# Routed layers: the last two experts' outputs stay on chip and are added by float32 products; the branch stands ahead of them

## The chip, the cores and the metric

One core of a Trainium2 chip. The program runs on that core alone; the time is the device time of one execution in microseconds (us), and the kernel before was run three times. TensorE (PE) multiplies, VectorE (DVE) and ScalarE (ACT) work on elements, GpSimd (POOL) and SyncE (SP) mostly issue DMAs here. Each engine works through its own instructions in order and waits on semaphores.

## What is computed

256 tokens of 1024 values pass a first block (feed-forward, retention and forgetting attention, feed-forward; two layers), and then a second block of two routed layers: `a` (window attention; 256 latent and 256 context tokens, 512 in all, four tiles of 128) and `b` (differential attention; 256 tokens, two tiles). After its attention each routed layer has a mixture of 16 experts, two for a token, a residual with `ALPHA`, and a layer norm:

```python
def moe_ffn(h, w_router, router_bias, w_gate, w_up, w_down):
    ...
    gates = (jax.nn.one_hot(eid, N_EXPERTS, dtype=F32) * w[..., None]).sum(1)
    out = jnp.zeros_like(h)
    for e in range(N_EXPERTS):
        y = (jax.nn.silu(h @ w_gate[e]) * (h @ w_up[e])) @ w_down[e]
        out = out + gates[:, e:e + 1].astype(h.dtype) * y
    return out
```

All weights are float32. A weight block of 128x1024 (0.5 MB) is used once.

## The kernel before

**The stream of weights.** `Stream` (L150 to 215) loads weight blocks in the order of their use. `_issue` starts a load into a buffer `raw` (SP's queue, L177), `_conv` makes two rounded halves of a block: `whi` by a cast on ACT (L189) and `wlo` by a subtraction on DVE (L191). `mm3` (L335 to 337) then multiplies three times: high by high, high by low, low by high. `DEPTHS` says by stage how many blocks may be in flight (`nraw`), converted and unreleased (`nhalf`), and converted ahead (`ahead`). `between()`, which products call between blocks, converts one block ahead and runs one piece of other work from the list `fill`. The order of instructions on each engine is the order in which the program is written.

**The routed experts.** `moe` routes the tokens, scatters their rows to `X` in memory by expert slots (`scatter`, L1733), and goes through the 16 experts in the order `ORDER[l]`. Experts are ranked by their number of tokens; a rank has a fixed number of slots (up to 256, down to 32), and tokens beyond them are overflow. For an expert, `xcol` multiplies its tokens with four blocks of the gate and four of the up weights; `folded` and `trans` turn the result into `uT`, `hth` and `htl`; its down product `Dn` (four blocks) runs one iteration later, so that the down product of an expert stands behind the gate and up products of the next. A small expert (64 or 32 slots) multiplies both of its halves at once (L1777, `mm<-whi,xt` and `mm<-wlo,xt`).

**How outputs reach the tokens.** `Dn` copies its accumulator to `y` (ACT, L1824) and stores it to `Y` in memory (L1825); the last expert in two halves (L1829, L1830). Then comes `overflow` (L1978, L1979): every engine loads the number of overflow blocks and branches. It is zero for these inputs, so each jumps over the block; SP, which waits in it for all of its DMA lanes, lets the others go on. Then `combine` has POOL gather each token's two rows from `Y` (`yr`, L1919), ACT scale the one by its gate (L1930), and DVE add the other with its gate (L1935), multiply by the row `g2` (L1936), add to `x` with `ALPHA` (L1939) and take the statistics (L1940). Thirteen small products make the layer norm's factors (L302 to 313, L1948, L1949). After layer a `attn_b` scales the first tile (L2046), transposes it, and goes on; after layer b `second` scales and shifts (L2232, L2236) and stores the result.

The inner part of the combination, before:

```python
            def both(c):
                a, b = y[i, 0], res["b"]
                V.scalar_tensor_tensor(a[:, c], a[:, c], g[:, 0, i:i + 1], b[:, c], op0=OP.mult, op1=OP.add)
                V.tensor_tensor(a[:, c], a[:, c], self.g2[t // 2][:, c], op=OP.mult)

            def added(c):
                V.scalar_tensor_tensor(x[:, c], x[:, c], ALPHA, y[i, 0][:, c], op0=OP.mult, op1=OP.add)
                V.bn_stats(st[:, c.start // 512, :], x[:, c])
```

Of the kernel before, what the change touches and what calls it, by code (L numbers as in the profile page):

```python
# [18 lines left out]
try:  # L19
# [38 lines left out]
def layout(pairs):  # L58
# [4 lines left out]
    for p, ranks in enumerate(pairs):  # L63
# [15 lines left out]
        for r, _ in ranks:  # L79
# [11 lines left out]

N4, N2 = 35, 21
# [6 lines left out]
          "route": ((6, 5, 5), (10, 5, 5)), "moe": ((6, 7, 5), (10, 7, 5)), "more": ((10, 11, 8), (11, 11, 8)), "end": (2, 6, 6)}  # L99
# [5 lines left out]
def host_constants():  # L105
    f = np.float32
    c = {}
    c["eye"] = np.eye(128, dtype=f)
    tri = (np.arange(128)[:, None] <= np.arange(128)[None, :]).astype(f)
    c["cum"] = np.concatenate([np.zeros((128, 128), f), tri, np.ones((128, 128), f)], 1)  # L110
    c["causal"] = np.where(tri.T > 0, f(0), f(NEG))
    inv = np.power(f(10000.0), -np.arange(0, 128, 2, dtype=f) / f(128))
    ang = np.arange(SEQ, dtype=f)[:, None] * inv[None, :]
    cs, sn = np.cos(ang), np.sin(ang)
    c["rope"] = np.stack([np.concatenate([cs, cs], 1), np.concatenate([-sn, sn], 1)], 1)
    lg = np.log1p(-np.exp2(-5.0 - np.arange(4)))
# [17 lines left out]
    c["rest"] = np.array(SLOTS)[:, None, None] + 128 * np.arange(8).reshape(2, 4) + np.arange(128)[:, None, None, None]  # L134
# [110 lines left out]
class Kernel:  # L245
# [647 lines left out]
    def zeros(self):  # L893

        z = self.k4([128, D], name="zero")
        self.nc.gpsimd.memset(z, 0.0)
        for x, m in zip(self.X, SLOTS):
            for a in range(0, m, 128):
                self.nc.gpsimd.dma_start(x[a:a + 128, :], z)
                yield  # L900
        for y, m, n, runs in zip(self.Y, SLOTS, MORE, RUNS):
            gaps = [(p * 256 + r[-1][0] + r[-1][1] * r[-1][2], p * 256 + 256) for p, r in enumerate(runs)]
            for a, b in gaps + [(m + a * 128, m + a * 128 + 128) for a in range(n)]:
                if a < b:
                    self.nc.gpsimd.dma_start(y[a:b, :], z[:b - a])
                    yield

    def ada_setup(self):
        self.mod = self.dr.tile([DEPTH, 2, 6, D], FT, name="mod")
        self.Y = [self.dr.tile([m + n * 128, D], FT, name=f"Y{m}") for m, n in zip(SLOTS, MORE)]  # L910

        self.X = [self.dr.tile([m + 1024, D], FT, name=f"X{m}") for m in SLOTS]
        self.H = [self.dr.tile([n, D], FT, name=f"H{n}") for n in (512, 256)]
# [470 lines left out]
    def attn_out(self, l, tiles, vec):  # L1384
# [84 lines left out]
        def second(oT):  # L1469
# [23 lines left out]
            def split(t):  # L1493
                self.split(h2[t][0], h2[t][1], hs[t])
                i = tiles.index(t)
                nc.gpsimd.dma_start(self.H[l][i * 128:i * 128 + 128, :], hs[t])
# [185 lines left out]
    def one_hot(self, r, i, c0, n, out):  # L1682

        V = self.nc.vector
        a = self.t([128, 256], "oha", bufs=2)
# [6 lines left out]
        V.scalar_tensor_tensor(out, self.iota[:, :n], rm[:, 1:2], a[:, :n], op0=OP.is_equal, op1=OP.add)  # L1692

    def moe(self, l, h2, hs):
# [30 lines left out]
        def scatter():  # L1725

            rows = self.t([128, 2, 4], "rtrow")[:, :, :T]
            V.tensor_tensor(rows, r, self.rest[:, l, :, :T], op=OP.min)
            ri = self.t([128, 2, 4], "rtrowi", I32)[:, :, :T]
# [72 lines left out]
        def stored(e, i, p, n):  # L1802
            hT[e, i] = (self.k2([128, 4, n], FR, name="hth"), self.k2([128, 4, n], FR, name="htl"))
            self.split(hT[e, i][0], hT[e, i][1], p)

        def Dn(e):
# [12 lines left out]
            for i, (c, n, _, _) in enumerate(ts):  # L1819
                rows = Y[p * 256 + c:p * 256 + c + n, :]  # L1820
                if e != seq[-1]:
# [3 lines left out]
                    S.dma_start(rows, y[:n])  # L1825
                else:
                    for x in range(2):
                        y = self.k2([128, 512], name="y")
                        S.copy(y[:n], b[i][x][:n])  # L1829
                        S.dma_start(rows[:, x * 512:(x + 1) * 512], y[:n])  # L1830
                del hT[e, i]

# [12 lines left out]
        for j, e in enumerate(seq):  # L1845
            p, ts = place[e][0], TILES[l][e]
            nxt = pairs[got] if j + 1 < len(seq) and got < len(pairs) and place[seq[j + 1]][0] == pairs[got] else None
            if j == len(seq) - 2:
                self.g2 = {v: self.modrow(l, v, 5) for v in range(T // 2)}
            if nxt is not None:  # L1850
# [45 lines left out]
            if last is not None or nxt is not None:  # L1896
                for i in range(len(ts)):
                    trans(i)
            else:
                self.fill.extend([lambda: None] + [lambda i=i, f=trans: f(i) for i in range(len(ts))])  # L1900
# [5 lines left out]
        if MORE[l] and not self.dbg.get("noov"):  # L1906
            self.overflow(l, Y)
        return g

    def combine(self, l, g):  # L1910
# [5 lines left out]
        for i in range(T):  # L1916
            for j in range(2):
                y[i, j] = self.k4([128, D], name="yr")
                nc.gpsimd.indirect_dma_start(out=y[i, j], out_offset=None, in_=self.Y[l],  # L1919
                                             in_offset=bass.IndirectOffsetOnAxis(ap=self.ri[:, j, i:i + 1], axis=0))  # L1920
        halves = [slice(0, 512), slice(512, 1024)]

        def pieces(i, t):
# [14 lines left out]
            def added(c):  # L1938
                V.scalar_tensor_tensor(x[:, c], x[:, c], ALPHA, y[i, 0][:, c], op0=OP.mult, op1=OP.add)  # L1939
                V.bn_stats(st[:, c.start // 512, :], x[:, c])  # L1940

            def norm():

                del y[i, 0], res["b"]
# [5 lines left out]
            p = [scaled]  # L1950
            for c in halves:
                p += [lambda c=c: both(c), lambda c=c: added(c)]
            return res, p, norm
# [20 lines left out]
    def overflow(self, l, Y):  # L1974
# [4 lines left out]
        with self.tc.If(n > 0):  # L1979
            oi = self.owners()  # L1980
            for a in range(MORE[l]):
# [3 lines left out]
                for i in range(T):  # L1985
                    self.one_hot(self.rt, i, first, 128, oh[:, i, :])
                x = [self.k2([128, 4, 128], name="ovx") for _ in range(2)]
                for f in range(2):
                    h = [self.k2([128, 512], name="ovt") for _ in range(T)]
                    for j in range(T):  # L1990
                        nc.sync.dma_start(h[j], self.H[l][j * 128:j * 128 + 128, f * 512:(f + 1) * 512])
# [34 lines left out]
    def attn_b(self, g):  # L2026
# [28 lines left out]
        comb = self.combine(0, g)  # L2055
# [18 lines left out]
        def ahead(n):  # L2074

            no = lambda: None
            first, rest, norm, done = ([lambda j=j: [f() for f in comb[j][1][0:3]] for j in range(4)],
                                       [lambda j=j: [f() for f in comb[j][1][3:5]] for j in range(4)],
                                       [lambda j=j: [f() for f in comb[j][2]()] for j in range(4)],
                                       [lambda j=j: finish(order[j], comb[j][0]) for j in range(4)])  # L2080
            step = lambda: hT[order[n + 1]].step()
            return ([lambda: (rest[1](), norm[1]()), first[2], done[1], rest[2], norm[2], step, step, done[2]],
                    [first[3], rest[3], step, step, norm[3]], [done[3], no, step, step], [])[n]

        (res, p, norm), p1 = comb[0], comb[1][1]
# [6 lines left out]
        p1[0]()  # L2092
# [3 lines left out]
        for f in p1[1:3]:  # L2096
# [118 lines left out]
    def second(self):  # L2215
# [5 lines left out]
        g = self.moe(0, *h2)  # L2221
        del h2
        h2 = self.attn_b(g)
        del self.xs[2:]
        g = self.moe(1, *h2)
        lg, lb = self.row(self.I["ln_ffn_g_2"][1:2, :]), self.row(self.I["ln_ffn_b_2"][1:2, :])
        comb = self.combine(1, g)
        (r0, p0, n0), (r1, p1, n1) = comb

# [10 lines left out]
        for f in p0 + p1[0:1]:  # L2240
            f()
        self.weave(n0(), p1[1:])
# [86 lines left out]
```

## Time and profile before

| | |
|---|---|
| runs, us | 2428.07, 2427.30, 2422.94 (median 2427.3) |
| the profiled execution | 2428.2 us; its span, from first to last instruction, 2426.4 |
| PE busy | 2204.8 us (91%) |
| DVE busy | 1830.1 us (75%) |
| ACT busy | 1269.2 us (52%) |
| POOL busy | 258.7 us (11%) |
| HBM read and written | 512.67 and 41.50 MB, 228 GB/s over the span |

Times in rows are microseconds from the start of the span. Experts of layer a run from about 1480 to 1800, those of layer b from about 2080 to 2392. In a row of the timeline stand the start, the busy time of a group of like instructions, the engine, the line and operation, what it writes and reads, how many, and in brackets how long the engine was idle before it and what ended that. A `q` behind an engine's name is its sequencer, which issues DMAs and branches.

### The profile page before, as it was taken

The numbers are of one execution on the slowest core, as the hardware profiler recorded it, in microseconds if no ns is written. First come the engines' busy times: TensorE is split into PE (matmuls) and PEld (weight loads), VectorE is DVE, ScalarE is ACT, GpSimd is POOL, SyncE is SP. The second block draws the span as 40 slices with busy tenths as digits, with TensorE's granted clock in tenths as the row PEclk, the third lists the DMA queues.
The fourth block names the chain that finished last, engine by engine and source line by source line (L and its number), as shares of the span: only waits on it lengthen the run. The fifth ranks groups of instructions, "written<-read, shape, count | busy, mean of one in ns | idle before, by whom it ended". The sixth has DMA issues, their size and how long they took to land. (4 is left out here: it accounts for less than half of the span.)

```text
span 2426.4 us, 32170 instructions
## 1 busy us (share of the span) xinstructions
PE 2204.8 (91%) x10767; PEld 1761.5 (73%) x10767; DVE 1830.1 (75%) x2700; ACT 1269.2 (52%) x1887; POOL 258.7 (11%) x600
## 2 busy tenths in 40 slices
PE   7999999999999999999998996999958977799994
PEld 5888787788788889788876775777637855576662
DVE  5787678877877766877667766989866486778896
ACT  4445444444444545444336614878855352577783
POOL 2003101100200301120100022000020011100000
PEclk9999999999999999999999996999989998799997
DMA  8786557779798676798711136999991410899994
GB/s 276 241 238 199 158 165 228 236 232 300 243 325 252 207 226 193 245 263 234 217 53 44 53 105 245 361 371 391 385 308 39 127 63 14 330 354 339 362 396 156
DMA packets 256448, 556.44 MB, mean 229 GB/s; under 512 B 23761, under 2 KB 43153, under 8 KB 256273
## 3 DMA queue, kind: packets, MB, share of 16 engines
q1 hardware_dynamic: 233248, 481.96, 61.1%
q0 software_dynamic: 17424, 57.78, 6.5%
q10 hardware_dynamic: 5601, 14.54, 1.6%
q8 instruction: 88, 1.44, 0.3%
q14 instruction: 87, 0.71, 0.1%
HBM read 512.67 MB, written 41.50 MB: 228 GB/s over the span
## 5 line engine op out<-in xcount | busy, mean ns | idle before, releaser
L191 DVE TENSOR_TENSOR wlo<-raw,whi 128x1024 fp32r<-128x1024 f32 (+1 forms) x828 | 975.7, 1210 | 188.4 <-ACT whi L189 177.0
L189 ACT CAST whi<-raw 128x1024 fp32r<-128x1024 f32 (+1 forms) x828 | 830.4, 1043 | 190.0 <-PE mm L336 56.0
L335 PE MATMUL mm<-whi,xth 128*128 128x512 f32 (+3 forms) x1152 | 446.4, 388 | 9.2 <-ACT whi L189 5.5
L337 PE MATMUL mm<-whi,xtl 128*128 128x512 f32 (+3 forms) x1152 | 432.4, 375 | 0.1
L336 PE MATMUL mm<-wlo,xth 128*128 128x512 f32 (+3 forms) x1152 | 431.5, 375 | 0.5 <-DVE wlo L191 0.5
L335 PE MATMUL acc<-whi,hth 128*128 128x512 f32 (+4 forms) x624 | 248.0, 397 | 7.4 <-ACT hth L367 7.4
L335 PEld LDWEIGHTS mm<-whi,xth 128*128 128x128 f32 x1152 | 218.6, 190 | 47.1 <-ACT whi L189 5.9
L337 PEld LDWEIGHTS mm<-whi,xtl 128*128 128x128 f32 x1152 | 218.3, 190 | 37.1 <-DVE xtl L368 1.7
L336 PE MATMUL acc<-wlo,hth 128*128 128x512 f32 (+4 forms) x624 | 245.0, 393 | 0.2 <-DVE wlo L191 0.2
L337 PE MATMUL acc<-whi,htl 128*128 128x512 f32 (+4 forms) x624 | 244.7, 392 | 0.0
L336 PEld LDWEIGHTS mm<-wlo,xth 128*128 128x128 f32 x1152 | 218.7, 190 | 32.8 <-DVE wlo L191 1.2
L965 DVE SCALAR_TENSOR_TENSOR adaacc<-adaraw,adac,adaacc 128x512 f32<-128x512 f32 x310 | 220.7, 745 | 13.5 <-DMA adaraw<-in_w_ada_dram 11.2
L335 PEld LDWEIGHTS acc<-whi,hth 128*128 128x128 f32 (+4 forms) x624 | 107.4, 172 | 41.2 <-ACT hth L367 7.6
L337 PEld LDWEIGHTS acc<-whi,htl 128*128 128x128 f32 (+4 forms) x624 | 107.3, 172 | 36.3 <-issue 0.8
L336 PEld LDWEIGHTS acc<-wlo,hth 128*128 128x128 f32 (+4 forms) x624 | 107.4, 172 | 34.0 <-DVE wlo L191 0.6
L1777 PE MATMUL mm<-whi,xt 128*128 128x512 f32 (+1 forms) x288 | 118.2, 410 | 10.3 <-ACT xt L1723 5.8
L306 POOL TENSOR_TENSOR rsw<-rsy 128x1 f32<-128x1 f32 (+1 forms) x75 | 26.1, 349 | 867.7 <-DVE rsy L304 850.1
L1777 PE MATMUL mm<-wlo,xt 128*128 128x512 f32 (+1 forms) x288 | 116.3, 404 | 2.1 <-DVE wlo L191 2.1
L367 ACT CAST hth<-tr 128x512 fp32r<-128x512 f32 (+3 forms) x64 | 35.4, 553 | 153.0 <-PE tr L363 147.3
L335 PE MATMUL mm<-whi,hth 128*128 128x512 f32 x256 | 105.1, 411 | 5.0 <-DVE x L497 2.8
L335 PE MATMUL mm<-whi,xt 128*128 128x512 f32 (+4 forms) x256 | 102.9, 402 | 3.3 <-ACT xt L367 3.3
L336 PE MATMUL mm<-wlo,xt 128*128 128x512 f32 (+4 forms) x256 | 101.9, 398 | 3.8 <-DVE wlo L191 3.7
(471 smaller groups left out, 3344.6 us busy)
## 6 DMA issues: line engine op xcount, KB each, us to landing
raw<-in_w_ffn_in_dram SPq DMA_DIRECT2D x176, 512.0 KB, 6.0
raw<-in_w_gate_dram SPq DMA_DIRECT2D x128, 512.0 KB, 8.4
raw<-in_w_up_dram SPq DMA_DIRECT2D x128, 512.0 KB, 7.1
raw<-in_w_down_dram SPq DMA_DIRECT2D x128, 512.0 KB, 8.5
adaraw<-in_w_ada_dram SPq DMA_DIRECT2D x384, 128.0 KB, 5.5
raw<-in_w_ffn_out_dram SPq DMA_DIRECT2D x88, 512.0 KB, 5.9
raw<-in_w_in_dram SPq DMA_DIRECT2D x56, 512.0 KB, 4.2
raw<-in_wqkv_b_dram SPq DMA_DIRECT2D x24, 512.0 KB, 7.6
```

The costliest lines, as they stand in the source:

```text
L189: k.nc.scalar.copy(hi, lo)
L191: k.nc.vector.tensor_tensor(low, lo, hi.bitcast(FT), op=OP.subtract)
L306: newton = [lambda: g.tensor_tensor(w, y, y, op=OP.mult), lambda: g.tensor_tensor(w, w, a, op=OP.mult), lambda: g.tensor_scalar(w, w, -0.5 ...
L335: mm(out, xh, wh, start=first, stop=False)
L336: mm(out, xh, wl, start=False, stop=False)
L337: mm(out, xl, wh, start=False, stop=last)
L367: self.nc.scalar.copy(hi, src)
L965: V.scalar_tensor_tensor(a, r[:, i, :], sc, a, op0=OP.mult, op1=OP.add)
L1777: PE.matmul(o[:2 * n], x[:, i, c:c + 2 * n], a[:, i, :], start=first and q == 0, stop=last and q == 1)
```

## The change

The last two experts of each layer (`LAST`: ranks 11 and 12 of layer a with 64 slots each, 14 and 15 of layer b with 32 each) don't go to `Y`.

- `scaled` multiplies their accumulators by the row `g2` into an on-chip tile `zy` (128 or 64 slots in all, DVE, L1865). `gated` builds for each tile of tokens a matrix with the token's gates at the slots of its experts (L1708 to 1712), which is transposed and copied to `zgT` (L1877). `product` multiplies `zgT` with `zy` in float32 (L2012), and `last` adds the product to `x` and takes the statistics (L2016, L2017).
- `overflow` now stands ahead of the second-last expert's iteration, with its block not on the straight path of the program.
- `combine` is called when the third-last expert's down product has been stored: POOL gathers for the first two tiles, and for tile `i + 2` when tile `i` is done. Scaling, gate, row and residual of these tiles (`first`) run from `fill` in the last expert's iteration. `attn_b` and `second` get `comb` and do the rest.
- `ORDER[0]` changes so that the four experts of 64 slots come last in layer a. From the third-last expert on the stream has the depths `z`, (5, 7, 5) and (6, 8, 6), instead of (10, 11, 8) and (11, 11, 8).
- `H` and its six stores go; the overflow block would gather from `X` instead. `X` is filled with zeros in full (12 more stores of 0.5 MB, and 2 of the gaps in `Y`, at the zeros' old place in the program).

```diff
-ORDER = ((15, 9, 0, 10, 11, 1, 12, 2, 3, 4, 5, 14, 7, 6, 13, 8),
+ORDER = ((15, 14, 0, 5, 1, 7, 2, 13, 3, 6, 4, 8, 9, 10, 11, 12),
          (4, 5, 0, 6, 7, 8, 1, 9, 10, 11, 2, 12, 3, 13, 14, 15))
+LAST = [o[-2:] for o in ORDER]
...
-          ... "more": ((10, 11, 8), (11, 11, 8)), "end": (2, 6, 6)}
+          ... "more": ((10, 11, 8), (11, 11, 8)), "z": ((5, 7, 5), (6, 8, 6)), "end": (2, 6, 6)}
...
+    def gated(self, r, g, i, c0, out):
+        V = self.nc.vector
+        rm, n = self.small(2, name="rm"), out.shape[-1]
+        V.tensor_scalar(rm, r[:, :, i], -float(c0), None, op0=OP.add)
+        a = [out, self.t([128, 256], "oha", bufs=2)[:, :n]]
+        for j in range(2):
+            V.tensor_scalar(a[j], self.iota[:, :n], rm[:, j:j + 1], g[:, j, i:i + 1], op0=OP.is_equal, op1=OP.mult)
+        V.tensor_tensor(out, out, a[1], op=OP.add)
...
-                rows = Y[p * 256 + c:p * 256 + c + n, :]
-                if e != seq[-1]:
+                if e in LAST[l]:
+                    scaled(p * 256 + c - z0, n, b[i])
+                else:
                     y = self.k4([128, D], name="y")
...
+        def scaled(o, n, b):
...
+                    V.tensor_tensor(Z["y"][v][o:o + n, c], b[x][:n], self.g2[v][o:o + n, c], op=OP.mult)
...
-            if j == len(seq) - 2:
+            if j == len(seq) - 3:
+                W.depth(*DEPTHS["z"][l])
                 self.g2 = {v: self.modrow(l, v, 5) for v in range(T // 2)}
+            if j == len(seq) - 2 and not self.dbg.get("noov"):
+                del ps, us, hs, trans, q
+                self.overflow(l, Y)
+            if j == len(seq) - 1:
+                self.fill.extend(places())
...
+            if j == len(seq) - 1:
+                self.drain()
+                self.fill.extend(comb[0][1])
             ps, hs = xcol(p, ts, W.next(4)), []
...
+            if j == len(seq) - 1:
+                self.fill.extend([lambda: None, lambda f=trans: f(0)] + comb[1][1])
             if last is not None:
                 Dn(last)
+                if j == len(seq) - 2:
+                    comb = self.combine(l, g, Z)
...
-        if MORE[l] and not self.dbg.get("noov"):
-            self.overflow(l, Y)
-        return g
+        return comb
...
+            def product(n):
...
+                nc.tensor.matmul(p, Z["gT"][:k, i], Z["y"][t // 2][:k, halves[n]], start=True, stop=True)
+
+            def last(n):
+                c = halves[n]
+                V.tensor_tensor(x[:, c], x[:, c], res["p"][n] if T == 2 else res["p"][:, n], op=OP.add)
+                V.bn_stats(st[:, n, :], x[:, c])
...
-        with self.tc.If(n > 0):
+        with self.tc.If(n > 0, preferred_fallthrough_block=False):
```

ACT at the end of layer b, before: the copies and the store of the second-last expert, those of the last in halves, the branch with the activations of the block that is jumped over (`u<-mm`), and the four scalings of the gathered rows.

```order
L1794 ACTIVATE uT<-fold 128x128
L189 CAST whi<-raw 128x1024
L1824 COPY y<-acc 32x512 x2
L1825 DMA Y_84<-y 32x1024
L367 CAST hth<-uT 128x128
L1829 COPY y<-acc 32x512
L1830 DMA Y_84<-y 32x512
L1829 COPY y<-acc 32x512
L1830 DMA Y_84<-y 32x512
L1978 TENSOR_LOAD rtnov
L1979 COMPARE_AND_BRANCH
L2008 ACTIVATE u<-mm 128x512 x7
```

The same place now, from the third-last expert's copies to the last cast but one; the block of the branch is ahead of it.

```order
L1851 DMA Y_84<-y 32x1024
L378 CAST hth<-uT 128x128
L200 CAST whi<-raw 128x1024 x4
L1877 COPY zgT<-tr 64x256
L1820 COPY gs<-mm 64x512
L200 CAST whi<-raw 128x1024
L1992 ACTIVATE yr<-yr,rtg 128x512 x2
L200 CAST whi<-raw 128x1024 x3
L1820 COPY gs<-mm 64x512
L1815 ACTIVATE uT<-fold 128x128
L200 CAST whi<-raw 128x1024 x2
```

The scalings, which were the last rows of the layer, stand among the casts; six casts (one more below) and a `gs` copy are behind the first two of them.

DVE at the end of layer b, before: the last conversions, and behind them the branch; the combining products all stand behind that.

```order
L368 TENSOR_TENSOR htl<-uT,hth 128x128
L191 TENSOR_TENSOR wlo<-raw,whi 128x1024 x8
L1795 SCALAR_TENSOR_TENSOR uT<-uT,fold 128x128
L191 TENSOR_TENSOR wlo<-raw,whi 128x1024
L1883 SCALAR_TENSOR_TENSOR uT<-fold,uT 128x128
L368 TENSOR_TENSOR htl<-uT,hth 128x128
L1978 TENSOR_LOAD rtnov
L1979 COMPARE_AND_BRANCH
```

DVE now, from the first row that combines to the products `zy` of the second-last expert.

```order
L1998 TENSOR_TENSOR yr<-yr,row 128x512
L2001 SCALAR_TENSOR_TENSOR x<-x,yr 128x512
L202 TENSOR_TENSOR wlo<-raw,whi 128x1024
L1816 SCALAR_TENSOR_TENSOR uT<-uT,fold 128x128
L202 TENSOR_TENSOR wlo<-raw,whi 128x1024 x2
L1940 SCALAR_TENSOR_TENSOR uT<-fold,uT 128x128
L379 TENSOR_TENSOR htl<-uT,hth 128x128
L202 TENSOR_TENSOR wlo<-raw,whi 128x1024
L1997 SCALAR_TENSOR_TENSOR yr<-yr,rtg 128x512
L1998 TENSOR_TENSOR yr<-yr,row 128x512
L2001 SCALAR_TENSOR_TENSOR x<-x,yr 128x512
L1865 TENSOR_TENSOR zy<-acc,row 32x512 x2
```

The combining products of a half (L1997, L1998, L2001) now stand between conversions, and each of them holds up the conversions behind it.

## Rows read from the trace of the kernel before

**Rows 1.** The page: GB/s moved in 40 equal slices of the span (60.7 us each).

```profile
GB/s 276 241 238 199 158 165 228 236 232 300 243 325 252 207 226 193 245 263 234 217 53 44 53 105 245 361 371 391 385 308 39 127 63 14 330 354 339 362 396 156
```

**Rows 2.** Windows: stretch, us, busy per engine (count), PEclk, DMA share, GB/s.

```profile
1480.00:1800.00 320.00, 288.68 (x1311) 215.71 (x1309) 274.15 (x287) 240.36 (x304) 27.04 (x57) 0.95 1.00 370
...
2340.00:2380.00 40.00, 40.00 (x191) 24.75 (x190) 37.47 (x38) 35.66 (x46) 1.59 (x3) 1.00 1.04 399
...
2390.00:2400.00 10.00, 1.25 (x6) 0.38 (x4) 0.00 (x0) 1.15 (x2) 3.86 (x4) 0.69 0.34 105
```

**Rows 3.** Timeline of PE, end of layer b.

```profile
2353.89 0.45 PE L1777 MATMUL mm<-whi,xt 128*64 128x512 f32 x1
...
2368.06 1.07 PE L1790 MATMUL fold<-fold,gs 64*128 64x32 f32 x8
```

**Rows 4.** Timeline of DVE, end of layer b.

```profile
2373.13 9.42 DVE L191 TENSOR_TENSOR wlo<-raw,whi 128x1024 fp32r<-128x1024 f32 x8 [0.66 <-ACT whi L189]
...
2384.85 0.28 DVE L1883 SCALAR_TENSOR_TENSOR uT<-fold,uT 128x128 f32<-128x128 f32 x1
...
2402.51 0.75 DVE L1935 SCALAR_TENSOR_TENSOR yr<-yr,rtg 128x512 f32<-128x512 f32 x1 [16.72 <-ACT yr L1930]
2403.30 0.69 DVE L1936 TENSOR_TENSOR yr<-yr,row 128x512 f32<-128x512 f32 x1
2404.03 0.69 DVE L1939 SCALAR_TENSOR_TENSOR x<-x,yr 128x512 f32<-128x512 f32 x1
...
2421.65 1.41 DVE L2236 SCALAR_TENSOR_TENSOR x<-x,rsy,row 128x512 f32<-128x512 f32 x2
```

**Rows 5.** Timeline of ACT, end of layer b.

```profile
2369.26 1.05 ACT L1824 COPY y<-acc 32x512 f32<-32x512 f32 x2
...
2401.76 1.33 ACT L1930 ACTIVATE yr<-yr,rtg 128x512 f32<-128x512 f32 x2 [9.63 <-DMA yr<-Y,rtri]
```

**Rows 6.** Timeline of POOL, end of layer b.

```profile
2395.02 1.02 POOL L1919 DMA_INDIRECT yr<-Y,rtri  x1 [18.69 <-SPq L1979]
2396.35 0.96 POOL L1919 DMA_INDIRECT yr<-Y,rtri  x1 [0.30 <-issue]
```

**Rows 7.** DMA issues, median us to landing, 2340 to 2400; the last row 1450 to 1520.

```profile
Y<-y ACTq DMA_DIRECT2D x3, 128.0 KB, 5.4
Y<-y ACTq DMA_DIRECT2D x2, 64.0 KB, 1.9
yr<-Y,rtri POOLq DMA_INDIRECT x4, 6.1
...
X<-h,rtrowi POOLq DMA_INDIRECT x8, 9.1
```

**Rows 8.** Line 1979, the branch: ns, first and last start; the last row 2350 to 2427.

```profile
L1979 SPq EVENT_SEMAPHORE  x18: 17/17/17, 1797.4 to 2394.2; - x18
...
L1979 SPq COMPARE_BRANCH  x2: 53/53/53, 1791.9 to 2370.7; - x2
L1979 DVEq COMPARE_BRANCH  x2: 63/68/72, 1795.5 to 2386.1; - x2
...
L1979 DVEq EVENT_SEMAPHORE  x2: 21/21/21, 1799.9 to 2386.7; - x2
...
L1979 SPq EVENT_SEMAPHORE  x9: 17/17/17, 2375.9 to 2394.2; - x9
```

**Rows 9.** Timelines, end of layer a: PE, DVE, ACT, PE.

```profile
1753.60 0.39 PE L337 MATMUL acc<-whi,htl 128*88 128x512 f32 x1
...
1818.69 0.21 DVE L1948 BATCH_NORM_AGGREGATE mv<-bnst 128x2 f32<-128x12 f32 x1
...
1821.44 1.24 ACT L2046 ACTIVATE ctx<-ctx,nmr,rsy 128x1024 f32<-128x1024 f32 x1 [4.17 <-DVE nmr L1949]
...
1822.73 1.97 PE L363 MATMUL tr<-ident,ctx 128*128 128x128 f32 x8 [22.37 <-ACT ctx L2046]
...
1843.66 0.50 PE L337 MATMUL mm<-whi,htl 128*128 128x512 f32 x1 [1.64 <-DVE htl L368]
```

More of the change, by code (lines that the diff above doesn't have):

```diff
@@ L90, with last_slots @@
 SLOTS = [len(p) * 256 for p in PAIRS]
+def last_slots(l):
+    (p, c, n), (_, d, m) = (PLACE[l][r] for r in LAST[l])
+    assert c + n == d
+    return p * 256 + c, n + m
 N4, N2 = 35, 21
@@ L897, in zeros @@
         for x, m in zip(self.X, SLOTS):
-            for a in range(0, m, 128):
+            for a in range(0, x.shape[0], 128):
                 self.nc.gpsimd.dma_start(x[a:a + 128, :], z)
                 yield
-        for y, m, n, runs in zip(self.Y, SLOTS, MORE, RUNS):
+        for l, (y, m, n, runs) in enumerate(zip(self.Y, SLOTS, MORE, RUNS)):
             gaps = [(p * 256 + r[-1][0] + r[-1][1] * r[-1][2], p * 256 + 256) for p, r in enumerate(runs)]
+            gaps.append((last_slots(l)[0], sum(last_slots(l))))
             for a, b in gaps + [(m + a * 128, m + a * 128 + 128) for a in range(n)]:
@@ L1824, in Dn, with places, one, turned @@
                         S.copy(y[:n, x * 512:(x + 1) * 512], b[i][x][:n])
[L1825 to L1830, printed above, removed]
-                del hT[e, i]
+                    S.dma_start(Y[p * 256 + c:p * 256 + c + n, :], y[:n])
+                del hT[e, i]
+        z0, nz = last_slots(l)
+        Z = {}
+        def scaled(o, n, b):
+            if "y" not in Z:
+                Z["y"] = [self.k4([128, D], name="zy") for _ in range(T // 2)]
+            for v in reversed(range(T // 2)):
+                for x in range(2):
+                    c = slice(x * 512, x * 512 + 512)
+                    V.tensor_tensor(Z["y"][v][o:o + n, c], b[x][:n], self.g2[v][o:o + n, c], op=OP.mult)
+        def places():
+            def one(i):
+                if i == 0:
+                    Z["g"] = self.k2([128, T, nz], name="zg")
+                self.gated(r, g, i, z0, Z["g"][:, i])
+            def turned():
+                p = self.transp([Z["g"][:, i] for i in range(T)])
+                Z["gT"] = self.k2([128, T, 128], name="zgT")
+                S.copy(Z["gT"][:nz], p[:nz])
+                del Z["g"]
+            return [lambda i=i: one(i) for i in range(T)] + [lambda: None, turned]
         for f in one_hots(pairs[0]):
@@ L1895, in moe @@
                 turn(nxt, 3)
-            if last is not None or nxt is not None:
+            if j < len(seq) - 1:
                 for i in range(len(ts)):
                     trans(i)
-            else:
-                self.fill.extend([lambda: None] + [lambda i=i, f=trans: f(i) for i in range(len(ts))])
             last = e
@@ L1915, in combine, with gather @@
         y = {}
-        for i in range(T):
+        def gather(i):
             for j in range(2):
@@ L1939, in added @@
                 V.scalar_tensor_tensor(x[:, c], x[:, c], ALPHA, y[i, 0][:, c], op0=OP.mult, op1=OP.add)
[L1940 removed]
+                if c.start:
+                    del y[i, 0], res["b"]
+                    if i + 2 < T:
+                        gather(i + 2)
+            def product(n):
+                if not n:
+                    res["p"] = [self.bank("acc", [128, 512], name="zp") for _ in halves] if T == 2 else \
+                        self.bank("s2", [128, 2, 512], name="zp")
+                p, k = res["p"][n] if T == 2 else res["p"][:, n], last_slots(l)[1]
+                nc.tensor.matmul(p, Z["gT"][:k, i], Z["y"][t // 2][:k, halves[n]], start=True, stop=True)
[3 more added lines that the diff above has]
+                V.bn_stats(st[:, n, :], x[:, c])
             def norm():
[L1944 removed]
                 mv, nm = self.small(2, name="mv"), self.small(1, name="nmr")
@@ L1949, in norm @@
                     [lambda: V.scalar_tensor_tensor(nm, mv[:, 0:1], -1.0, r, op0=OP.mult, op1=OP.mult)]
-            p = [scaled]
+            first = [scaled]
             for c in halves:
-                p += [lambda c=c: both(c), lambda c=c: added(c)]
-            return res, p, norm
+                first.append(lambda c=c: (both(c), added(c)))
+            return res, first, [lambda n=n, f=f: f(n) for f in (product, last) for n in range(2)], norm
         return [pieces(i, t) for i, t in enumerate(self.order)]
@@ L1989, in overflow @@
                     h = [self.k2([128, 512], name="ovt") for _ in range(T)]
+                    two, ri = self.t([128, 4], "ovr")[:, :T], self.t([128, 4], "ovri", I32)[:, :T]
+                    V.tensor_scalar(two, self.rows[:, 0, :], 2.0, float(f), op0=OP.mult, op1=OP.add)
+                    V.tensor_copy(ri, two)
                     for j in range(T):
-                        nc.sync.dma_start(h[j], self.H[l][j * 128:j * 128 + 128, f * 512:(f + 1) * 512])
+                        nc.gpsimd.indirect_dma_start(
+                            out=h[j], out_offset=None, in_=self.X[l].rearrange("r (a c) -> (r a) c", a=2),
+                            in_offset=bass.IndirectOffsetOnAxis(ap=ri[:, j:j + 1], axis=0))
                     b = self.bank("acc", [128, 4, 128], name="ovg")
@@ L2091, in attn_b @@
         W.eng = nc.sync
-        p1[0]()
+        for f in p1[:2]:
+            f()
         for f in norm():
@@ L2095, in attn_b @@
         finish(order[0], res)
-        for f in p1[1:3]:
+        for f in p1[2:]:
             f()
```

55 lines of the change are left out of this document (29 added, 26 removed).

## The prediction, made before the change was run

> **What bounds the kernel now.** I read the slices of the page first: the two routed layers are the two stretches at 300 to 396 GB/s [rows 1]. The windows then show two regimes. While a layer's experts run, TensorE and the loads are both full: the 320 us of layer a's experts move 370 GB/s at a DMA share of 1.00, and the last full 40 us of layer b have PE busy for 40.00 us with DVE at 37.47 and ACT at 35.66 [rows 2]. PE, DVE and the loads stand within some per cent of each other. Then all of it stops: in 2390 to 2400 PE is busy for 1.25 us and DVE for nothing [rows 2]. That stop is what the change is about. The last expert's outputs go to memory, all engines pass the branch, POOL gathers, ACT and DVE combine: POOL waits 18.69 us for SP's end of the branch [rows 6], ACT waits 9.63 us for the gathered rows [rows 5], and DVE's first combining product comes after 16.72 us of idleness [rows 4]. From it to the end of the last shift stand 20.55 us of DVE work (2402.51 to 2423.06) [rows 4]. The stop after layer a is like it: PE idles for 22.37 us until it can transpose the first normalized tile [rows 9].
>
> **What is to be won.** If gathers and combining products run while the last two experts do, of DVE's 20.55 us in layer b the four scalings and row products with 0.75 + 0.69 us each [rows 4] leave the tail, and the tail no longer holds a store, a branch and a gather. They don't vanish: DVE does them between conversions, in a stretch where it is busy for 37.47 of 40 us [rows 2].
>
> **Layer b, step by step.** t0 is the end of the down product of the third-last expert, 2368.1, where the next fold starts [rows 3]; no weight load is removed, so I leave it there. The branch now stands one expert ahead, about 14.2 us before t0 (gate and up from 2353.89) [rows 3].
> The path to the gathered rows: two copies 1.05 us [rows 5] and the issue, 1.5 together. Landing of that store: 1.9 us by the two that went alone, 5.4 under load [rows 7]; I take 2.5, since SP's wait in the branch has just emptied the queue. Then 0.4 for the wait, the second gather 1.33 after the first [rows 6], and 6.2 to land, between the quiet gathers at 6.1 and the scatters under load at 9.1 [rows 7]. Sum: t0 + 11.9. The ends are t0 + 11.3 and t0 + 17.7 (5.4, and 9.1 plus a us of queueing).
> ACT comes to the scalings at about t0 + 8 (in its order 17 casts stand between branch and scalings, and three copies). So it waits there some 4 us: a new wait, in order, and behind it stand six casts and the `gs` copy from which PE's last fold is made. DVE from the branch to that point has 17 conversions of 1.18 us (9.42 for eight [rows 4]), small products and two tiles of gates; no row has the gate products at 64 columns, the nearest is 0.28 for 128x128 [rows 4], so 1 us a tile, between 0.5 and 2. That is 24 us in the 26 us up to t0 + 11.9: hidden, with 2 us of cover.
> From the rows' landing DVE is the chain: scaling 1.33 [rows 5], one cast 1.0, six conversions 7.3, four times (0.75 + 0.69 + 0.69) 8.7, four `zy` products of an accumulator with the gate row at 0.69 [rows 4] 2.8, three small ones 0.9, short waits of the kind of 0.66 [rows 4] 0.8: 22.8. The float32 product has no row: 0.39 if it ran like the others of 512 columns; 2.1 if like the folds, eight float32 products of 32 columns in 1.07 us [rows 3], so 512 columns at 2.1. I take 1.0; PE is idle there. The rest of the old tail is 20.55 less the four 1.44 or 5.8: 14.7. End: t0 + 11.9 + 22.8 + 1.0 + 14.7 = t0 + 50.4, where it was 2423.06, t0 + 55.0. **Minus 4.6.**
>
> **Layer a.** The loads bind there, so the branch is reached where the matching down product ended, 1754 [rows 9], up to 3.6 us later because two small experts have taken the place of two large ones; I take 1755. Then t0 is 15.1 later (14.2 as in layer b, and 0.9 for wider folds), the rows land at t0 + 11.9, and DVE has until the first transposes: scaling and cast 2.3, thirteen conversions 15.3, four combining triples 8.7, eight `zy` 5.5, small ones and waits 2.2, the two adds and statistics 2.8, the norm 2.75 (1818.69 to 1821.44) and the scaling of the tile 1.24 [rows 9]: 41. Transposes at 1755 + 15.1 + 11.9 + 41 = 1823.0, against 1822.73 [rows 9]. Afterwards one gap of 1.64 us [rows 9] should go, since the second tile is further on. **Minus 1.3.** Layer a gives little because its conversions, once the cover of its wait, now stand in its chain.
>
> **The branch.** It is what can take all of this back. Before, it stood where everything was stopping. DVE's jump took 4.4 us in layer a (1795.5 to 1799.9) and 0.6 in layer b (2386.1 to 2386.7), SP's 5.5 in layer a (1791.9 to 1797.4) and 5.2 in layer b (2370.7 to 2375.9) [rows 8], all beside the wait for the store. Now DVE pays in its chain. I take 0.5 a layer, layer b's value, because fewer loads are in flight (five or six blocks instead of ten or eleven), with 4.4 as the upper end. SP waits in its block for every outstanding load (some 8 us for six blocks at 1.3 us, 0.52 MB by 399 GB/s [rows 2]) and then jumps, so no load is issued for some 13 us. Nine and eleven blocks are landed or in flight then, and DVE needs 1.2 us for one. In layer b the 17 blocks after it would all have landed at 13.4 + 4 + 16 x 1.3 = 38 us after the branch, converted at 40; DVE takes up its last one at about 42. In layer a, with 19 blocks, both stand at 43. So this is covered by 2 us and by nothing.
>
> *By the skill.* The Trainium skill, "Runtime: NRT & Kernel Launch", section "Instruction fetch mechanics", says that a taken branch whose target lies outside the two fetched pages must wait for a DMA fetch of the target. It speaks against a branch in mid-stream, where the fetch has to come in beside the loads; the 4.4, 5.5 and 5.2 us agree with it, layer b's 0.6 on DVE does not show it. The sum by it is that of rival 1.
>
> **What costs nothing.** The removed `H` stores and the 14 zero stores more lie in earlier stages (the zeros' is that of the tenth and eleventh slice) where DMA has room, at 300 and 243 GB/s [rows 1]; if that cover were gone a zero store of 0.5 MB would cost 1.3 us. Two stores of outputs a layer go: some 0.26 MB each, under 1 us of the loads, not counted.
>
> **Sum.** -4.6 - 1.3 + 2 x 0.5 = -4.9 on the profiled execution's 2428.2 gives 2423.3; it stands 0.9 above the median of 2427.3, so **2422**.
>
> **Rivals.**
> 1. *The branch in mid-stream costs more than it frees: slower.* DVE pays 4.4 us in each layer instead of 0.5 (+7.8), and SP's jump of 5.5 lets the loads restart late, 2 us past the cover in layer a and 1 in layer b. -4.9 + 7.8 + 3 = +6, 2433; with both jumps under full load up to 2440. For it: the three long jumps of the trace were taken beside loads. Against: DVE's 0.6. It decides from 5 us of loss over the two layers on. Chance 0.25.
> 2. *The gathers land late.* At t0 + 17.7 in place of 11.9 ACT stands for 10 us and the casts with it: +5.8 a layer. The gain is gone, and more: about 2431 with one layer and a half of it. For it: 9.1 us for scatters under load. Against: the queue is shallow then. Chance 0.12.
> 3. *No wait at all.* If the rows are there when ACT comes (t0 + 8), each layer gains 4 to 4.5 more and DVE is without a pause from the branch on: 2413. Chance 0.18.
> 4. *The thinner stream starves PE.* Five or six blocks in flight for three experts; a small expert asks for 12 blocks in 14.2 us, 443 GB/s, and got 399. If PE slips by 2 us a layer the change does not do what it says: 2427. Chance 0.07.
> The forecast has the remaining 0.38, its own range 2416 to 2429.
>
> **How the numbers follow.** 0.2%, about 5 us, is what a measurement of this kernel tells from no change. Faster than 2422.4: half of the forecast's 0.38, all of rival 3, and some of the others, 0.44. Within: a good third of the forecast, half of rivals 2 and 4, a little of rival 1, 0.29. Slower: most of rival 1, half of rival 2, 0.27. The range from 2410 to 2438 leaves out some of rivals 1 and 3.
>
> **What would show it.** Right: POOL's gathers issued some 4 us after t0, an ACT idle of about 4 us at the scalings, DVE without gaps from there to the end, 14.7 us from the first add to the last shift. DVE's jump at 0.5 says forecast; at 4 it says rival 1, and so does a hole of over 15 us in the loads after either branch. Wrong would be a DVE that idles behind the scalings, or a layer a whose transposes start several us off 1823 with the branch not at 1755.

## The result, and the profile after

The changed kernel takes 2464.1 us (median of four; one of them, at 3575 us with a granted clock of 0.58, is left out of comparisons). Its ratio to the kernel before is 1.0143, interval 1.0117 to 1.0168: slower by some 35 us. The forecast was 2422, range 2410 to 2438. The profiled execution has a span of 2463.4 us, 37.0 more than before.

Both programs convert 828 weight blocks in the same stages, so the end of the same `wlo` in the two traces tells where the time went (a count over DVE's timeline, from 0, in us; the differences are taken before rounding):

```
conversion    before    after     later by   what lies there
340           1047.6    1048.0      0.4      end of the first block
360           1104.8    1117.6     12.9      start of the second block
420           1501.0    1513.9     12.8      layer a, its experts begin
640           2084.3    2113.8     29.5      layer b, its experts begin
800           2349.2    2381.3     32.2      layer b, third-last expert
end of span   2426.4    2463.4     37.0
```

Three losses, then: 12.5 us at 1100, where the forecast had nothing; 16.7 in layer a, where it had -0.8; and in layer b 2.7 on the way and 4.9 at its end, where it had -4.1. These are differences of single executions. In the stretch from 640 to 800, which no later edit touches, the fourteen other traces of changed kernels are 0.6 to 5.1 us later than this trace of the kernel before, so the 2.7 have no cause that is shown here, and a difference of 2 or 3 us between two traces is not read as an effect.

**The first loss.** The waits of the kernel after, 1040 to 1120 (engine and line, what it waited for, us in total, times, longest):

```profile
ACT hth L378 <- DMA Y<-zero: 14.9, 1, 14.9
DVE htl L379 <- ACT hth L378: 13.9, 4, 11.9
...
PE mm L346 <- DVE sa L477: 10.7, 1, 10.7
```

A cast of the second block waits for a store of zeros, DVE for the cast, PE for DVE. The rows of the tensors that the zero tile fills, after (ns, first and last start), and POOL's timeline:

```profile
L910 POOL DMA_DIRECT2D X<-zero x34: 533/533/606, 547.9 to 972.7; - x34
L917 POOL DMA_DIRECT2D Y<-zero x18: 524/543/607, 973.3 to 1080.6; - x18
```

```profile
1068.84 3.85 POOL L917 DMA_DIRECT2D Y<-zero  x7
1073.74 0.53 POOL L917 DMA_DIRECT2D Y<-zero  x1 [1.05 <-DMA mod<-adab]
```

The zeros are issued one at a step of the first block's work. There are 41 such steps, enough for the 38 stores of before and not for 52. The other 11 go out in a burst when the second block begins (`self.zero.get()`), and the cast that reuses the zero tile's buffer waits until the last has landed, at 1097.4.

**The branch.** Line 2055 of the kernel after, layer b (ns min, median, max; first and last start), against [rows 8] and against PE's row of the same view before, which [rows 8] leaves out; then PE's and DVE's timelines there:

```profile
L1979 PEldq COMPARE_BRANCH  x2: 3534/3722/3911, 1796.3 to 2387.4; - x2
```

```profile
L2055 SPq EVENT_SEMAPHORE  x9: 17/17/17, 2382.1 to 2389.4; - x9
...
L2055 PEldq COMPARE_BRANCH  x2: 81/2342/4603, 2383.1 to 2386.3; - x2
...
L2055 DVEq COMPARE_BRANCH  x2: 47/54/61, 2387.7 to 2387.9; - x2
```

```profile
2390.91 0.69 PE L1798 MATMUL mm<-whi,xt 128*64 128x512 f32 x1 [4.85 <-DVE wlo L202]
2391.40 0.63 PE L1798 MATMUL mm<-wlo,xt 128*64 128x512 f32 x1
```

```profile
2388.56 4.63 DVE L202 TENSOR_TENSOR wlo<-raw,whi 128x1024 fp32r<-128x1024 f32 x4 [1.51 <-ACT whi L200]
2397.87 4.63 DVE L202 TENSOR_TENSOR wlo<-raw,whi 128x1024 fp32r<-128x1024 f32 x4 [4.68 <-ACT whi L200]
```

DVE's jump is short here (2387.9 to a conversion at 2388.6). PE's is not: its second branch begins at 2386.25, lasts 4.6 us, and the next product starts at 2390.91, when the four gate blocks that it needs had been converted since 2384.9. SP waits for its loads until 2389.4 and jumps; between a load issued at 2381.0 and the next at 2392.2 there is none, a hole of 11.2 us.

In layer a DVE's jump is long too. Line 2055 there, then ACT's and DVE's timelines:

```profile
L2055 PEldq COMPARE_BRANCH  x2: 98/2251/4404, 1767.3 to 1770.1; - x2
```

```profile
1772.65 3.88 ACT L200 CAST whi<-raw 128x1024 fp32r<-128x1024 f32 x4 [1.64 <-ACTq L2055]
1775.43 4.63 DVE L202 TENSOR_TENSOR wlo<-raw,whi 128x1024 fp32r<-128x1024 f32 x4 [3.96 <-ACT whi L200]
```

DVE's second branch ends at 1772.3 and its next instruction starts 3.1 us later, though the first of the four casts was done at 1773.7. PE, whose jump of 4.4 us ends at 1774.6, works then on blocks converted before, so DVE's jump lies beside PE's.

**The gathers.** Timelines of ACT and POOL after, end of layer b, against [rows 5, 6]:

```profile
2384.42 1.26 ACT L1851 COPY y<-acc 128x512 f32<-128x512 f32 x2 [0.47 <-PE acc L348]
...
2405.97 1.27 ACT L1851 COPY y<-acc 32x512 f32<-32x512 f32 x2 [0.62 <-PE acc L348]
...
2422.26 1.33 ACT L1992 ACTIVATE yr<-yr,rtg 128x512 f32<-128x512 f32 x2 [5.91 <-DMA yr<-Y,rtri]
```

```profile
2412.97 1.03 POOL L1979 DMA_INDIRECT yr<-Y,rtri  x1 [44.09 <-DMA raw<-in_w_down_dram]
2414.30 1.13 POOL L1979 DMA_INDIRECT yr<-Y,rtri  x1 [0.30 <-issue]
```

t0, just ahead of the copies at 2405.97, comes 21.6 us after the copies ahead of the branch (14.2 forecast). The gathered rows are there 16.3 us after t0 (11.9 forecast): from the store's issue to POOL's first gather 5.7 us pass, and the second gather takes 7.9. From there DVE needs 37.7 us to its last shift at 2460.0, 38.5 forecast.

### The profile page after: what moved, and what is told of

Same layout as the page of the kernel before. It is cut to its first block, busy times and chain, and to the rows that moved or that the text cites. A ratio compares the mean times of both kernels' runs of the same rounds, so it can differ in the third digit from the quotient of the medians.

```text
span 2463.4 us, 32274 instructions
## 1 busy us (share of the span) xinstructions
PE 2231.6 (91%) x10797; PEld 1775.4 (72%) x10797; DVE 1853.1 (75%) x2748; ACT 1267.8 (51%) x1881; POOL 267.5 (11%) x612
## 5 line engine op out<-in xcount | busy, mean ns | idle before, releaser
L346 PE MATMUL acc<-whi,hth 128*128 128x512 f32 (+5 forms) x608 | 241.9, 398 | 2.8 <-ACT hth L378 2.8
L347 PE MATMUL acc<-wlo,hth 128*128 128x512 f32 (+5 forms) x608 | 238.8, 393 | 0.0
L348 PE MATMUL acc<-whi,htl 128*128 128x512 f32 (+5 forms) x608 | 238.8, 393 | 0.0
L976 DVE SCALAR_TENSOR_TENSOR adaacc<-adaraw,adac,adaacc 128x512 f32<-128x512 f32 x310 | 220.7, 745 | 14.3 <-DMA adaraw<-in_w_ada_dram 14.3
L1798 PE MATMUL mm<-whi,xt 128*128 128x512 f32 (+1 forms) x288 | 125.9, 437 | 28.9 <-DVE xt L379 13.2
L346 PEld LDWEIGHTS acc<-whi,hth 128*128 128x128 f32 (+5 forms) x608 | 105.6, 174 | 35.7 <-ACT hth L378 3.8
L348 PEld LDWEIGHTS acc<-whi,htl 128*128 128x128 f32 (+5 forms) x608 | 105.3, 173 | 34.8 <-issue 1.5
L347 PEld LDWEIGHTS acc<-wlo,hth 128*128 128x128 f32 (+5 forms) x608 | 105.6, 174 | 32.2 <-DVE wlo L202 0.7
L1798 PE MATMUL mm<-wlo,xt 128*128 128x512 f32 (+1 forms) x288 | 123.1, 427 | 3.0 <-DVE wlo L202 3.0
L348 PE MATMUL mm<-whi,htl 128*128 128x512 f32 x256 | 101.8, 398 | 1.6 <-DVE htl L379 1.6
```

The costliest lines, as they stand in the source:

```text
L346: mm(out, xh, wh, start=first, stop=False)
L347: mm(out, xh, wl, start=False, stop=False)
L348: mm(out, xl, wh, start=False, stop=last)
L976: V.scalar_tensor_tensor(a, r[:, i, :], sc, a, op0=OP.mult, op1=OP.add)
L1798: PE.matmul(o[:2 * n], x[:, i, c:c + 2 * n], a[:, i, :], start=first and q == 0, stop=last and q == 1)
```

## The experiments

Ratios are to the kernel before, on the same chip; medians in us.

**Zeros early** (`e1`): two stores of `X` at a step.

```diff
                 self.nc.gpsimd.dma_start(x[a:a + 128, :], z)
-                yield
+                if a % 256:
+                    yield
```

> The 52 zero stores all stay, but two of those to X go out at each step, so that none is left over at the start of the second block. Theory (a scalar cast of the second block takes the buffer of the zeros and waits 14.9 us for the last late store): 12.5 us less than the changed kernel, about 2451.5, and that wait is gone. Rival (the stores cost by their 7 MB more of traffic): no gain, 2464.

2463.7, ratio 1.0143 (1.0125 to 1.0162): no gain, the number of the rival. The wait of the cast is gone and all zeros are issued by 981, yet the trace is 8.1 us late at conversion 340. That came between 550 and 740; from 570 to 730 DVE now waits 23.5 us for the `adaraw` loads:

```profile
DVE adaacc L977 <- DMA adaraw<-in_w_ada_dram: 23.5, 7, 8.9
```

It was 14.3 us after the change, and 11.2 before. The edit moved the loss instead of removing it: packed, the zeros crowd the loads of a stretch that is nearly full. The window of the kernel before and that of `e1` (the last two numbers are the DMA share and GB/s):

```profile
560.00:745.00 185.00, 181.55 (x864) 149.64 (x863) 152.05 (x192) 82.17 (x97) 20.02 (x49) 1.00 0.92 284
560.00:745.00 185.00, 175.56 (x822) 144.31 (x821) 142.17 (x181) 77.21 (x93) 26.40 (x61) 0.98 0.96 316
```

**Zeros short** (`e5`): only the 12 stores more to `X` taken back.

```diff
-            for a in range(0, x.shape[0], 128):
+            for a in range(0, m, 128):
```

> Only the 12 zero stores more to the rows of X that the overflow block alone would read are taken back (those rows are then not zeroed); the two stores for the gaps stay. 40 stores fit into the 41 steps that the changed kernel had. Theory: no late store, no packed stores, 12 us less than the changed kernel, about 2452. Rival (the run with packed stores gave the whole cost of the traffic): no gain, 2462.

2452.4, ratio 1.0094 (1.0077 to 1.0111): 12 us less. Conversion 400 is 0.6 us from its time before. Lateness of the stores and crowding of the loads are the two ways in which the same 12 stores cost some 12 us.

**No branch** (`e2`), and with zeros early (`e3`).

```diff
-            if j == len(seq) - 2 and not self.dbg.get("noov"):
-                del ps, us, hs, trans, q
-                self.overflow(l, Y)
```

> The changed kernel without the branch and its overflow block, which is left out of the computation. Theory (the branch in mid-stream costs 5.7 us a layer on the way from the branch to the end of the third-last expert's down product, 20 us instead of 14 to 15): 11 to 12 us less, about 2452.5, with no hole in the loads. Rival (the late gathers set the end and would have hidden the branch): 3 us less or nothing, 2461 to 2464.

> Both edits of the two runs before, the overflow block is left out. Theory: the two add up, 24 us less than the changed kernel, about 2440, which is still above the kernel before by what the late gathers and the rest of the two ends cost. Rival (with the branch gone the gathers stay as late as they were): 2449.

2450.0 (1.0094) and 2447.8 (1.0078). Without the branch the copies of the two experts stand as close as the forecast had them, 15.2 us in layer b:

```profile
2372.93 1.27 ACT L1851 COPY y<-acc 128x512 f32<-128x512 f32 x2 [0.48 <-PE acc L348]
2388.12 1.26 ACT L1851 COPY y<-acc 32x512 f32<-32x512 f32 x2 [0.36 <-PE acc L348]
```

So the branch costs 6.4 us on that way in layer b, and 7.5 in layer a (22.5 to 15.0). In layer b PE's idleness of 4.85 and 1.5 us by which its 32 products behind it are slower make up the 6.4. The end of layer b is then 4.0 us faster than before. The sum of the two edits fell short, since the first of them moved its loss.

**Late** (`e4`, with zeros early): scalings and combining products in and behind the last down product.

```diff
-                self.fill.extend(comb[0][1])
...
-                self.fill.extend([lambda: None, lambda f=trans: f(0)] + comb[1][1])
+                self.fill.extend([lambda: None, lambda f=trans: f(0)])
...
         self.drain()
+        self.fill.extend(comb[0][1] + comb[1][1])
         Dn(last)
+        self.drain()
```

> Zeros early, branch where the change has it, but the scalings of the gathered rows and the combining products run in the last down product and behind it, not among the conversions. Theory (ACT stands 5.9 us in layer b and 3.5 us in layer a for the gathered rows with six casts behind it, and DVE and PE stand with it): casts no longer wait, 5 to 8 us a layer less than the run with zeros early alone, about 2438. Rival (DVE's work is the chain whichever order it has): the same as with zeros early alone, 2451.

2448.2 (1.0081), 15.5 us less than `e1`. In the traces layer a gains 6 us and the end of layer b 8: ACT no longer stands for gathered rows with casts behind it. On short zeros the same edit gives 7 us and not 15 (`e5` to `e8`, below); why half is not known.

**Short zeros and late, without and with the branch** (`e6`, `e8`), and a different order of layer a (`e7`).

> The zeros of the run before this one, the combination behind the last down product, no branch (the overflow block is left out). Theory (the three losses add up: zeros 12, branch 9 a layer, scalings among the casts 6 to 8 a layer): some 40 us less than the changed kernel, 2420 to 2425, faster than the kernel before by a few us. Rival (late scalings and the branch hide each other, since both hold up the same conversions): 2432 to 2438.

> Zeros as in the first of these runs, the combination behind the last down product, and the branch where the change has it. Theory (additive): about 2437, 18 us more than without the branch. Rival (what the branch holds up is no longer waited for when the combination is last): 2428.

> As the run before this one, with layer a in an order near the old one, (15, 9, 0, 10, 1, 2, 3, 4, 5, 14, 7, 6, 8, 13, 11, 12), so that small experts again lie between large ones. Theory (the new order costs nothing, since the loads bind there): the same within 2 us. Rival (with the four small experts in a row at the end the loads and DVE fall behind, and the turns of the pairs wait on DVE for 12 us): 4 to 8 us less.

`e6` takes 2428.2, ratio 0.9998 (0.9988 to 1.0007); `e8` 2445.1, 1.0062. The branch is 17 us on this form. The additive 2420 to 2425 was missed. A wait that the forecast does not have is left in `e6`, PE in layer a:

```profile
PE tr L374 <- DVE zg L1712: 7.4, 4, 1.9
```

PE's transposes of the gate matrices stand in its order among the products and wait for DVE, which builds the matrices behind its conversions. The changed kernel has this wait too, 6.6 us, but there it lies ahead of the wait for the gathered rows. `e7`, at 2432.5 (1.0016), is 4 us slower: the change's order of layer a is not a loss.

**Gate matrices one expert earlier** (`e9`, on `e6`; the temporary is in another pool).

```diff
-            if j == len(seq) - 1:
-                self.fill.extend(places())
+            if j == len(seq) - 2:
+                self.fill.extend(places()[:T])
+            if j == len(seq) - 1:
+                self.fill.extend(places()[-1:])
```

> As the run with late combination and no branch, with the gate matrices built one expert earlier, so that their transposes find them ready (temporary in another buffer). Theory (PE's transposes of the gate matrices stand in its order among the products and wait for DVE, 7.4 us in layer a and 2 to 3 in layer b): 6 to 9 us less than that run, 2420, and faster than the kernel before. Rival (DVE bounds that stretch with or without the wait): the same, 2428.

2423.7, ratio 0.9990 (0.9979 to 1.0001). The wait is gone, but the gain is not clear of noise: 4.5 us less than `e6` by the medians, of two chips, 2 by the ratios, whose intervals overlap. At least part of the wait has moved, since DVE now builds the matrices in the expert before (its copies stand 21.1 us apart in layer a instead of 16.6). Layer a still costs 2.8 us in this trace and the end of layer b gives 9.8.

**What in the branch costs it.** `e10` (on `e8`): the block's DMAs, and the load of its expert's number, on POOL, so that SP has none to make up for. `e12`: in addition one overflow expert in the block instead of eight or seven.

```diff
-                        nc.sync.dma_start(w, wv[:, k, :])
+                        nc.gpsimd.dma_start(w, wv[:, k, :])
...
-            for a in range(MORE[l]):
+            for a in range(1):
```

> As the run with short zeros, late combination and the branch in its place, but the overflow block's loads and stores, which are jumped over, are issued by POOL and not by SP; so SP has no DMA in the block to make up for and does not wait for its outstanding loads. Theory (of the 7 us a layer the larger part is the hole in the loads): no hole over 6 us, 8 to 12 us less than that run, 2435. Rival (PE's jump of 4.5 us and the wait of all engines for the count are the price): 2 us less or nothing, 2443 to 2446.

> As the run with the overflow block's DMAs on POOL, but the block that is jumped over holds one overflow expert in place of eight (layer a) or seven (layer b); the rest is left out. Theory (PE's jump over its part of the block, 6.4 and 6.2 us in that run, is the branch's whole price, and it is long because the block is): PE's jump under 1 us, 12 to 14 us less than that run, about 2428. Rival (the price is the wait of all engines for the count and the meeting of their queues, whatever the block's length): the same, 2439 to 2441.

2441.0 (1.0059, 1.0041 to 1.0078) and 2439.2 (1.0047, 1.0030 to 1.0063). Both theories missed by their number: `e10` is where `e8` was (1.0062), and `e12` is 2 us below `e10`, where 12 to 14 were expected. In `e10` SP's two branches stand 0.1 us apart and it issues a load 0.4 us after the second; its wait for the loads is gone, though after four more loads it stands 7.8 us for PE, and the copies in layer b are still 24.0 us apart. PE has taken over, as line 2056 of `e10` and PE's timeline show:

```profile
L2056 SPq COMPARE_BRANCH  x2: 34/36/38, 2368.4 to 2368.5; - x2
L2056 PEldq COMPARE_BRANCH  x2: 81/3162/6243, 2369.5 to 2372.7; - x2
```

```profile
2378.98 0.69 PE L1798 MATMUL mm<-whi,xt 128*64 128x512 f32 x1 [6.49 <-DVE wlo L202]
```

With the short block of `e12` that jump is 0.3 us and the copies are 18.4 us apart:

```profile
L2056 PEldq COMPARE_BRANCH  x2: 64/185/306, 2365.2 to 2368.4; - x2
```

The copies say 5.6 us less in layer b and the medians do not, so two more pairs were run: `e11` and `e13` are all edits with the full and with the short block; `e14` is `e5` with the short block alone.

> Both edits of the two runs before, on the run with short zeros, late combination and the branch. Theory (additive): about 2427, the time of the kernel before. Rival (PE's jump stays): 2436.

> As the run with all edits (short zeros, late combination, gate matrices early, overflow on POOL), with one overflow expert in the block and the rest left out. Theory (PE's jump of 5 to 6 us a layer is in every execution): 8 to 10 us less than that run, a ratio of 0.999 to 1.000. Rival (what is not the jump sets the time, or DVE's work does): the same ratio as that run within 0.1%, 1.0025 to 1.004.

> The changed kernel with the short zeros, and in the block one overflow expert instead of eight or seven; the rest is left out. Theory (jump of PE 4.4 to 4.6 us and of SP in each layer): 8 to 10 us less than with the short zeros alone, about 2443. Rival (the hole in the loads, which SP's wait for its outstanding loads makes, is the price here, and it stays): the same, 2451 to 2453.

`e11` 2433.8 (1.0034, 1.0022 to 1.0047), where the additive 2427 was expected and its rival, that PE's jump stays, had 2436; `e13` 2426.0 (0.9995, 0.9985 to 1.0005): 7.8 us for the block's length by the medians, 9.5 by the ratios. So with SP's loads kept going the long jump has a price of some 8 us. It is not PE's alone: the short block shortens DVE's jump in layer a too (5.5 us in `e11`, 0.2 in `e13`), and no run separates the two there. Nor is it the whole price of the branch on its way: in `e13` the copies of layer b are 18.3 us apart, against 15.6 without a branch in `e9`.

`e14` 2454.7 (1.0107, 1.0091 to 1.0123): nothing, against `e5`, the number of its rival. In its trace the copies are 3.3 us closer than in `e5` in both layers (19.4 against 22.8 in layer b), and four casts behind the branch of layer b wait 2.9 us for loads, where in `e5` none does. So the hole, covered by PE's jump in the change's own form, comes out in part when the jump goes. Why the time has none of the 3 us is open.

**What PE waits for in its jump.** The packed traces hold the DMA packets of the instruction queues. In each of the 16 long jumps of PE (3.5 to 6.9 us, the kernel before, the change, `e1`, `e4`, `e5`, `e8`, `e10`, `e11`) one packet of 16384 bytes of the queue q8 starts and ends inside the jump, and the jump is over 1.3 to 1.5 us after it. In the six short ones (`e12` to `e14`, 0.3 to 0.4 us) there is none. From the jump's start to that packet's start it is 1.0 and 1.6 us in the kernel before, 2.1 to 2.5 where SP waits meanwhile and issues no load, and 3.7 to 4.5 in `e10` and `e11`, where it goes on. That fits `e10`, in which the hole was gone, PE's jump was longer and the time was the same.

No version with the whole computation beat the kernel before, and none of the others did clear of noise. A branch among the first experts, where the loads are the bound, was not tried.

## Why the prediction was wrong

- **The zeros.** "What costs nothing" failed. I looked at GB/s where the zeros began, and not at how many steps were left to issue them, nor at who takes their buffer next. 12 us.
- **The branch.** "I take 0.5 a layer" failed; it was 6.4 and 7.5. I counted DVE's jump and SP's. PE's stood in the same view of the kernel before, at 3.5 and 3.9 us, beside the last down product, which was still running; ahead of an expert it has no such cover. DVE's jump, which I had made the sign to look for, was 0.6 as taken in layer b, and the loss came all the same; in layer a it was 3.1, near rival 1's 4.4, but beside PE's longer one. Rival 1 had the place right and the wrong engine. The hole in the loads was not over 15 us but 11.2, below the 13 of the forecast, and SP's jump was 2.5, not 5.5. "Covered by 2 us and by nothing" holds in the change's own form only because PE stood longer: in `e14` casts wait for loads.
- **The gathers.** "I take 2.5" for the store, and 0.4 for the wait, was 5.7 in layer b and 7.5 in layer a; 6.2 for the gather was 7.9 and 7.8. Rival 2's t0 + 17.7 was nearly the case, 16.3 in layer b and 17.9 in layer a. The loads had already started again when the store went out.
- **Layer b, rest.** From the landing to the end 37.7 us against 38.5: the sum of DVE's work was right. With the way from the branch to t0 (6.9 more than taken, 5.9 for the branch and 1.0 for the expert itself, which takes 15.2 without a branch), the gathers (4.4), this (-0.8) and an earlier start (-1.6, the copies ahead of the branch reckoned from conversion 800) the end of layer b comes to 8.9 more than forecast; 9.0 was measured.
- **Layer a.** The branch was reached at 1755.6 on before's scale, 1755 forecast. Then the way to t0 6.9 more than taken, gathers 6.0, DVE 1.2 (42.2 against 41), and after the transposes 2.9, as the gap of 1.64 that I counted as won is still there (1.56) and 1.2 more were lost: 17.6 with the 0.6 at the start, 17.5 measured.
- **What the form allows.** `e9`, without branch, with other zeros and combinations late, is 3.4 us below the kernel before by the medians, within noise of nothing (0.9979 to 1.0001), against the 5 of the forecast. In its trace the end of layer b gives more than expected and layer a costs, and of the two only layer b's 9.8 is clear of the scatter between traces.

The float32 product was priced at 1.0 us. Its rows in layer b (ns min, median, max) show two records for each of the four products; the first add begins at 2444.84, 1.16 us after the first of them:

```profile
L2012 PE MATMUL zp<-zy,zgT x8: 589/934/1057, 2443.7 to 2448.2; 64*128 64x512 f32 x8
```

The Trainium skill, "Runtime: NRT & Kernel Launch", section "Instruction fetch mechanics", had the rule that a taken branch out of the fetched pages waits for a fetch. The runs agree for PE: 3.5 to 6.9 us over the long block, with an instruction packet in each jump, and 0.3 to 0.4 over the short one, with none. DVE agrees in layer a: 3.1 to 5.7 us from its second branch to its next instruction over the long block, 0.2 over the short one; in layer b it is 0.5 and 0.2. ACT shows no such wait in the middle of the stream (0.1 to 0.4).

## What to carry to other kernels

Before a branch is moved, read its price for each engine by itself, the idle ones too, and in each place by itself: what stood in the shadow of a stop comes into the chain when the stop goes. A step that is spread over other work by a counter has a last place; if more is added, ask where the rest falls and whose buffer it holds. And an early gather puts an in-order wait into the engine that consumes it: let it be consumed where nothing urgent stands behind.

## What was not expected of the hardware

- PE's jump over a block of the program, among loads, takes 4.4 to 6.9 us, the longest where the loads go on; over a block with one overflow expert 0.3 to 0.4. DVE's takes 3.1 to 5.7 us in layer a.
- The stop at the branch costs a second time. Behind it a product of 512 columns takes 0.63 us, against 0.39 ahead: the granted clock has gone to the lower of its levels (1.2 GHz; 0.50 from 2391 to 2394), after 4.85 us of idleness. Over the 20 us it is 0.83 (windows of the kernel after; PEclk is the third number from the end):

```profile
2340.00:2380.00 40.00, 40.00 (x187) 27.56 (x185) 37.16 (x37) 35.93 (x46) 0.53 (x1) 1.00 1.04 395
2380.00:2400.00 20.00, 15.15 (x64) 9.81 (x63) 13.41 (x15) 12.99 (x17) 0.00 (x0) 0.83 0.66 240
```

- A stretch at 284 GB/s, far below the 399 elsewhere, but at a DMA share of 0.92, took 12 stores of 0.5 MB only at a price: it went to 316 GB/s and 0.96, and what follows was 8 to 13 us late in the three traces that have them packed.
